# One encoder step in an order written out by a planner: first weight loads with places of their own, a margin for deferrable products, and measured durations in the planner's model

## The chip, the cores and the metric

The kernel runs on one core of a Trainium2 chip. The metric is the device time of that core in microseconds (us), as the median of several runs; the profile is one further execution, taken with the hardware profiler. TensorE (PE) multiplies, VectorE (DVE), ScalarE (ACT) and GpSimd (POOL) work on rows, SyncE (SP) issues all transfers.

## The reference, cut to what matters

One layer for 512 prompt tokens and 32 sample tokens, with 256 memory tokens, all in 32-bit floats. There are three head groups: A attends to a band of chunks, B to the highest-scored keys only, M to the memory. Cut down, for one sequence:

```python
def layer(x, mem, g, w_in, w_mem_kv, w_out, pos):
    z = _rmsnorm(x, g) @ w_in                       # 1024 -> 3880 columns, split:
    qa, ka, va, ga, qb, kb, vb, gb, qm, gm, qi, ki, wi = _split_cols(z)
    qb, kb, qi, ki = rope(qb), rope(kb), rope(qi), rope(ki)
    mk, mv = split(_rmsnorm(mem, g_mem) @ w_mem_kv)
    oa = softmax(qa @ ka.T / 8 + rel_bias) @ va     # 6 heads x 64, own chunk and 8 before
    score = sum_h(wi[h] * relu(qi[h] @ ki.T))       # 8 heads x 32, one shared key
    top = top_k(score, 128)                         # prompt; 256 for the sample
    ob = softmax(qb @ kb[top].T / 8) @ vb[top]      # 6 heads x 64
    om = softmax(qm @ mk.T / 8) @ mv                # 4 heads x 64
    o = concat(oa * silu(ga), ob * silu(gb), om * silu(gm))
    return _rmsnorm(x + o @ w_out, g_final)         # and all new keys and values
```

The sample attends to cached keys (1024 rows for B, 512 for A) beside its own 32.

## The kernel before, in words

Each product of the projections is done as three products of rounded halves: the inputs are split into a high and a low part (xTh, xTl; wh, wl), and TensorE adds wh·xTh, wh·xTl and wl·xTh in one bank. A weight piece arrives by a transfer (raw, four places), ACT rounds it (wh), POOL subtracts (wl). The 32 sample rows are done straight from raw and xF (w_sample), with no split.

Nothing is scheduled by a compiler: the Python program lays down every engine's instructions in the order in which they shall run. A class Line keeps a modelled clock for each engine and for the transfers, with a duration for each operation (cost, L62), a lag between engines (lag, L87) and the time at which each tile is written (had). The steps of the kernel are generators; each yields the model's time at which it wants to go on, for instance `line.at(tile)` (L169), the time at which the tile is ready plus a margin of 0.3. Between the products of the big projections (EARLY, then LATE, then out_part) the planner runs every generator whose time has come on TensorE's modelled clock. So the projections are the filler, and the other steps go in where the model says that their inputs are there. All operations go through one wrapper and therefore carry the same line, L233; they are told apart by the names of their tiles.

The steps that matter here: `start` (L656) issues the first transfers in the order of the string START (w: allow one more weight piece, x: a piece of x turned, t: the tables for rotation, r: 128 rows of x in natural order for the norms, m: memory). w_load (L409) lets a weight piece into one of four places when the piece four before it has been split. rows_load (L590) has two places for the rows (nat) and waits for the norm of the rows two before. norms gives rs, one over the root mean square of each row, on which the sparse branch and every rotation hang. `index` (L752) starts the sparse branch when all rows are normed: index_sample and index_prompt turn keys and queries (rot, stk, KS, QS; KSs, QSs for the sample), multiply them, and add the eight heads on VectorE (ysel for the prompt, ysS for the sample). picks then takes the 128 highest of each prompt row in 48 pairs of MAX8 and MATCH_REPLACE on VectorE. sample_choice finds the 256th highest score of each sample row by 22 rounds of trial: VectorE writes trial values (bi_neg, later bf_try), ACT counts what lies above (junkS, then bf_ok), TensorE adds up the counts (bank<-bf_ok,over), and VectorE takes the next digit (bi_ok, later bf_m and bf_cut). The last six rounds (bf_) settle ties. Group B's attention needs picks and choice; its products and the whole output projection come behind them.

The order of a queue is fixed, so an instruction that waits holds up all those behind it on its engine.

Of the kernel before, what the change touches and what calls it, by code (L numbers as in the profile page):

```python
# [17 lines left out]
P = 128  # L18
S = 512
# [16 lines left out]
START = "wxwxwxwtwwrrrrwwrmmrr"  # L36
# [7 lines left out]
class Line:  # L44
# [4 lines left out]
    def __init__(self):  # L49
        self.clk = dict.fromkeys(("PE", "DVE", "ACT", "POOL", "SP", "DMA"), 0.0)  # L50
        self.ready, self.used = {}, {}
        self.boxes = {}
        self.tables = {"exp": (AF.Exp, AF.Tanh)}
        self.table = None
        self.tasks = []
        self.seq = 0
        self.margin = 0.3
        self.time = 0.0
        self.window, self.busy, self.slow = 0.0, 0.0, True
        self.warm = None  # L60

    def cost(self, eng, op, outs, ins, kw):  # L62
        if eng == "PE":
            w = 1 if ins[0].dtype in (F32R, BF16) else 2 if op == "transpose" else 4
            n = outs[0].free_size() * w / 2400.0
            if op == "matmul" and ins[0].dtype == F32R:
                return 0.003 + max(n, 0.104) if "tile_position" not in kw else 0.02 + 0.5 * max(n, 0.104)
            if "tile_position" in kw:
                return 0.04 + n * (0.25 if outs[0].shape[0] == T else 0.5)
            return 0.003 + n  # L70
# [16 lines left out]
    def lag(of, to):  # L87

        if of == to or of is None:
# [49 lines left out]

    def op(self, eng, op, outs, ins, kw):  # L140
# [3 lines left out]
        if eng == "SP":  # L144
            self.clk[eng] = t + 0.05
            t = max(t + 1.1, self.clk["DMA"])
            end = t + outs[0].size() * 4 / 360e3
            self.clk["DMA"] = end
        else:
            d = self.cost(eng, op, outs, ins, kw)  # L150
            if eng == "PE":
                d = self.array(t, d)
            end = t + d
# [15 lines left out]
    def at(self, *tiles):  # L169
        return max(self.had(x) for x in tiles) + self.margin  # L170

# [91 lines left out]
def hybrid_step(ctx: ExitStack, tc: tile.TileContext, a: dict):  # L263
# [47 lines left out]
    ka = cp.tile([P, NT, 384], F32, tag="ka", name="ka")  # L311
    va = cp.tile([P, NT, 384], F32, tag="va", name="va")
# [6 lines left out]
    ysS = cp.tile([P, PAST + T], F32, name="ysS")  # L319
# [125 lines left out]
    def w_sample():  # L445
        for nm, i, n in parties:
            yield from line.wait(lambda: len(raws) > i + 1 and x_done[0] > 1)
            yield line.at(xF[:, 0:4, :], raws[i + 1])
            yield from room()
            p = bank()  # L450
            for j in (0, 2):
                yield from line.wait(lambda: len(raws) > i + j + 1 and x_done[0] > j + 1)
                yield line.at(raws[i + j], raws[i + j + 1], xF[:, 2 * j:2 * j + 4, :])
# [4 lines left out]
            yield line.at(p)  # L458
            if nm in ("kb", "vb"):
                yield from line.wait(lambda: 0 in over)  # L460
            out = (cp.tile([T, 384], F32, tag={"kb": "kaS", "vb": "vaS"}.get(nm, nm + "S"), name=nm + "S") if nm != "i"
                   else ix.tile([T, n], F32, name="zS"))
            A.copy(out, p[0:T, 0:n])
            for q in range(1, 4):
                yield line.at(out) - 0.2
                V.tensor_tensor(out, p[q * T:(q + 1) * T, 0:n], out, op=ALU.add)
            give(p)
            yield from line.wait(lambda: NT in normed)
            yield max(line.at(rs[0:T, NT:NT + 1]), line.at(out) - 0.2)
            V.tensor_scalar(out, out, rs[0:T, NT:NT + 1], None, op0=ALU.mult)  # L470
            news[nm] = out
            if nm in ("kb", "qb"):
                rope(out.rearrange("p (h d) -> p h d", d=64), out, T, 6, 64, ctab["cos64S"], ctab["sin64S"], V)
# [116 lines left out]
    def rows_load():  # L590
# [27 lines left out]
    def spread():  # L618

        yield from line.wait(lambda: NT in normed)  # L620
        yield line.at(rs)
# [130 lines left out]
    def index():  # L752
        nonlocal ip, identR
        yield from line.wait(lambda: len(indexed) == NT and NT in normed)
        p1.close()
        ip = pool(ipx, "ip", "right")
        identR = ip.tile([P, P], F32R, name="identR")
        V.tensor_copy(identR, ident)
# [39 lines left out]
    def index_prompt():  # L798
# [5 lines left out]
        yield line.at(kst)  # L804
# [7 lines left out]
        for t in range(1, NT):  # L812
            n = P * (t + 1)
            yield line.at(qst[t])
# [11 lines left out]
            yield line.at(QS)  # L826
# [16 lines left out]
    def index_sample():  # L843
# [14 lines left out]
        yield line.at(qsS)  # L858
# [14 lines left out]
        yield line.at(kst2)  # L873
# [5 lines left out]
        for k0, n in ((0, 512), (512, 512), (1024, T)):  # L879
            yield line.at(KSs)  # L880
# [7 lines left out]
            yield line.at(*rs)  # L888
# [33 lines left out]
    def sample_choice():  # L922
# [13 lines left out]
        def passed(of, bias, least_, scale=1.0):  # L936
# [4 lines left out]
            yield line.at(okf) - 0.2  # L941
# [137 lines left out]
    natural = {"ka": ka, "va": va}  # L1079

    def projections(order):
        for nm in order:
# [17 lines left out]
            else:  # L1100
                if nm not in natural:

                    line.until(lambda: (2 if nm == "kb" else 0) in over)
                    natural[nm] = cp.tile([P, NT, 384], F32, tag=nm, name=nm)
                of = f"new_{nm[1]}_{nm[0]}"
# [3 lines left out]
    def sample(mix, nh, nb, kt, cv, qT, kn, vn, pts, zin):  # L1109
# [6 lines left out]
        if kn is not None:  # L1116
            yield line.at(kn)
# [7 lines left out]
        yield line.at(qT, *kt)  # L1125
        yield from room(3)
        o_ps = bank()
        for g0 in range(0, nh, 4):
# [35 lines left out]
            yield line.at(z)  # L1164
# [18 lines left out]
            yield line.at(*(x[0] for x in blocks))  # L1183
            yield line.at(*cv)
# [94 lines left out]
    def turned_pair(nat, hp, then):  # L1279

        w = nat.shape[1] * P
        yield line.at(nat[:, :, hp * P:(hp + 1) * P])
# [55 lines left out]
    class Masked:  # L1338
# [57 lines left out]
        def turn(self):  # L1396
            pts = []
            for e in range(2):
                yield from line.wait(lambda: places[self.w] > 0)
                places[self.w] -= 1  # L1400
                yield line.at(self.z[e])
# [41 lines left out]
    def attend(i):  # L1443
# [9 lines left out]
        yield line.at(*pair.q, *pair.k)  # L1453
# [12 lines left out]
        yield line.at(*pts)  # L1466
# [220 lines left out]
```

## Time and profile before

| | us |
|---|---|
| median of 3 runs | 384.17 (383.58 to 387.33) |
| the profiled execution | 385.51 |
| its span in the trace | 383.7 |
| TensorE busy | 362.8 (95%) |
| VectorE busy | 286.1 (75%) |
| ScalarE busy | 224.5 (59%) |
| GpSimd busy | 186.1 (49%) |

The share of busy time is a mean over stages that have different limits, so it is to be read stage by stage. Matmuls of TensorE overlap, so a stage's busy time is the union of them, and the duration of one is read from the distance between starts. The mean granted clock of TensorE is 0.984 of full speed (2.4 GHz); its lower level is 1.2 GHz.

### The profile page before, as it was taken

Reading aid. Unit: us, or ns where it says so; the run is one execution under the profiler, and the core shown is the slowest. Engines: PE = TensorE matmul, PEld = TensorE weight load, DVE = VectorE, ACT = ScalarE, POOL = GpSimd, SP = SyncE. Lnnn points to the kernel's source line nnn. Section 1 sums busy time; section 2 is a strip of 40 time slices with the busy share of each in tenths; the row PEclk is TensorE's granted clock in tenths of the full one; section 3 lists DMA queues with packets and bytes.
Section 4 is the critical chain, followed back from the end, with each engine's and each line's share of the span. In section 5 each row is a group of like instructions: output and inputs, shape, how many; then the busy total and the mean of one; then the engine's idle time right before and its main releaser. Section 6 shows DMA issues by size and latency. Waiting matters only on the chain.

```text
span 383.7 us, 7976 instructions
## 1 busy us (share of the span) xinstructions
PE 362.8 (95%) x2961; PEld 324.6 (85%) x2961; DVE 286.1 (75%) x721; ACT 224.5 (59%) x529; POOL 186.1 (49%) x199
## 2 busy tenths in 40 slices
PE   8997889999999999999898999799999999999992
PEld 8795768999989888898697888799999877999992
DVE  3664877988999999999999997787755587422453
ACT  5664946898677777756475674323654556411353
POOL 1778862377433665416668623735224310633552
PEclk9999989999999999999998999989999999999998
DMA  7969641156564422112401220522145940230005
GB/s 248 309 209 290 194 140 58 61 172 186 166 205 141 124 72 57 42 42 80 114 24 61 85 63 27 164 56 55 43 156 195 370 167 2 78 140 4 0 15 219
DMA packets 41478, 46.35 MB, mean 121 GB/s; under 512 B 5184, under 2 KB 36544, under 8 KB 41440
## 3 DMA queue, kind: packets, MB, share of 16 engines
q1 hardware_dynamic: 41440, 45.85, 38.0%
q8 instruction: 23, 0.38, 0.4%
q14 instruction: 15, 0.12, 0.1%
HBM read 39.67 MB, written 6.16 MB: 119 GB/s over the span
## 4 chain that ended last, share of the span: by engine, by line
PE 67%; DVE 21%; DMA 5%; ACT 3%; issue 2%; SPq 1%; POOL 1%; POOLq 0%; DVEq 0%; ACTq 0%
PE bank L233 67%; DVE ysel L233 3%; DVE m L233 2%; DMA g_mem<-in_norm_mem_g_dram 2%; DVE z L233 2%; DMA raw<-in_w_in_dram 2%; DVE rank L233 1%; DVE st L233 1%; DVE rt L233 1%; DVE qbS L233 1%; SPq L233 1%; DMA cbi<-in_cache_b_kidx_dram 1%; DVE kbS L233 1%; ACT sq L233 1%; DVE rot L233 1%
## 5 line engine op out<-in xcount | busy, mean ns | idle before, releaser
L233 POOL TENSOR_TENSOR wl<-raw,wh 128x512 fp32r<-128x512 f32 (+2 forms) x68 | 107.7, 1592 | 116.0 <-ACT wh L233 105.6
L233 ACT ACTIVATE wh<-raw 128x512 fp32r<-128x512 f32 (+2 forms) x70 | 49.5, 715 | 43.4 <-PE bank L233 18.1
L233 PE MATMUL bank<-wh,xTh 128*128 128x384 f32 (+1 forms) x192 | 67.9, 354 | 0.0
L233 PE MATMUL bank<-wl,xTh 128*128 128x384 f32 (+1 forms) x192 | 64.9, 338 | 1.8 <-POOL wl L233 1.7
L233 PE MATMUL bank<-wh,xTl 128*128 128x384 f32 (+1 forms) x192 | 64.7, 337 | 0.0
L233 ACT ACTIVATE z<-z,st 128x256 f32<-128x256 f32 (+3 forms) x73 | 39.0, 548 | 23.9 <-DVE st L233 23.9
L233 PE MATMUL bank<-xTh,wh 128*128 128x272 f32 x208 | 46.5, 304 | 0.4 <-DVE st L233 0.4
L233 PEld LDWEIGHTS bank<-wh,xTh 128*128 128x128 f32 x192 | 37.3, 194 | 7.4 <-issue 6.5
L233 PE MATMUL bank<-xTl,wh 128*128 128x272 f32 x208 | 43.0, 288 | 0.0
L233 PE MATMUL bank<-xTh,wl 128*128 128x272 f32 x208 | 42.9, 288 | 0.0
L233 PEld LDWEIGHTS bank<-wl,xTh 128*128 128x128 f32 x192 | 37.2, 194 | 2.6 <-POOL wl L233 2.2
L233 PEld LDWEIGHTS bank<-wh,xTl 128*128 128x128 f32 x192 | 37.3, 194 | 0.4 <-DVE xTl L233 0.3
L233 PEld LDWEIGHTS bank<-xTh,wh 128*128 128x128 f32 x208 | 32.6, 189 | 3.1 <-issue 1.8
L233 PEld LDWEIGHTS bank<-xTl,wh 128*128 128x128 f32 x208 | 32.6, 188 | 0.0
L233 PEld LDWEIGHTS bank<-xTh,wl 128*128 128x128 f32 x208 | 32.6, 189 | 0.0
L233 PE MATMUL bank<-ident,z 128*128 128x128 f32 (+1 forms) x161 | 26.0, 281 | 1.7 <-ACT pt L233 1.1
L233 DVE TENSOR_TENSOR xr<-bank,xr 128x256 f32<-128x256 f32 (+1 forms) x24 | 12.3, 512 | 19.8 <-PE bank L233 19.7
L233 DVE MAX8 m<-ysel 128x8 f32<-128x256 f32 (+2 forms) x48 | 26.3, 548 | 0.0
L233 DVE MATCH_REPLACE8 ysel<-m,ysel 128x256 f32<-128x256 f32 (+2 forms) x48 | 26.0, 543 | 0.0
L233 PEld LDWEIGHTS bank<-ident,z 128*128 128x128 f32 (+1 forms) x161 | 18.0, 142 | 5.8 <-issue 2.1
L233 ACT ACTIVATE junkS<-ysS,bi_neg 128x1056 int8<-128x1056 f32 x16 | 18.8, 1177 | 3.6 <-DVE bi_neg L233 3.6
L233 ACT COPY pt<-bank 128x512 f32<-128x512 f32 (+1 forms) x28 | 14.8, 539 | 8.8 <-PE bank L233 8.7
(308 smaller groups left out, 902.2 us busy)
## 6 DMA issues: line engine op xcount, KB each, us to landing
raw<-in_w_in_dram SPq DMA_DIRECT2D x20, 384.0 KB, 3.5
raw<-in_w_in_dram SPq DMA_DIRECT2D x26, 256.0 KB, 2.9
raw<-in_w_out_dram SPq DMA_DIRECT2D x8, 384.0 KB, 3.2
nat<-in_x_prompt_dram SPq DMA_DIRECT2D x4, 512.0 KB, 5.3
raw<-in_w_mem_kv_dram SPq DMA_DIRECT2D x8, 256.0 KB, 2.8
xr<-in_x_prompt_dram SPq DMA_DIRECT2D x4, 512.0 KB, 5.6
out_dram<-xr SPq DMA_DIRECT2D x4, 512.0 KB, 2.6
xr<-in_x_t_dram SPq DMA_DIRECT2D x3, 544.0 KB, 6.1
```

Source lines behind the costliest of these rows:

```text
L233: return fn(*args, **kw)
```

## The change

- START has four weight pieces (w) ahead of the prompt's rows (r) instead of two. The first four pieces get places of their own (in the later places of q0 and gate0), and pieces below the eighth wait for no split. The rows from the third on get places of their own instead of taking turns in two; the tiles ka, va and ysS, whose places they use, are opened later (two waits in `projections` and `index` for that).
- `line.sure` (ready plus 1.0) stands in place of `line.at` (ready plus 0.3) before products of TensorE that nobody needs at once: in w_sample, spread, the indexer, the attention, and the rounds of the choice. A free bank is taken 0.4 later.
- What w_sample does behind its product goes into a generator of its own.
- The model: other durations for TensorE's operations, with one for a change of the array's division; VectorE and POOL wait for each other in the model where both use the port that they share; a transfer is given 1.6 instead of 1.1 before it lands and 330 instead of 360 GB/s.

```diff
-START = "wxwxwxwtwwrrrrwwrmmrr"
+START = "wxwxwxwtwwwwrrrrrmmrr"
+SURE = 1.0
...
-            n = outs[0].free_size() * w / 2400.0
-            if op == "matmul" and ins[0].dtype == F32R:
-                return 0.003 + max(n, 0.104) if "tile_position" not in kw else 0.02 + 0.5 * max(n, 0.104)
...
+            n = outs[0].free_size()
+            fast = ins[0].dtype in (F32R, BF16)
+            if op == "transpose":
+                d = max(0.085 if fast else 0.109 * ins[0].shape[0] / P, 0.06)
+            elif fast:
+                d = max(n / 2400.0 + 0.013, 0.107 if n > 1 else 0.04)
+            else:
+                d = 2 * max(n / 1190.0, 0.058)
...
+            if mode != self.mode:
+                self.mode = mode
+                d += 0.095 + (0.104 if fast else 0.056) * mode[1] / P
...
+    def port(self, eng, t, d):
+
+        for s, end, by in self.taken:
+            if by != eng and s <= t < end:
+                t = end
+        self.taken = [x for x in self.taken[-40:]] + [(t, t + d, eng)]
+        return t
...
+    def sure(self, *tiles):
+
+        return max(self.had(x) for x in tiles) + SURE
...
-            t = sorted(pp.free(f"b{b}") for b in free_banks)[k - 1]
+            t = sorted(pp.free(f"b{b}") for b in free_banks)[k - 1] + 0.4
...
-            yield from line.wait(lambda: allowed[0] > i and len(split) > i - 4 and (i - 4 not in party or i - 4 in met))
-            yield wp.free("raw")
-            raw = wp.tile([P, nk, hi - lo], F32, tag="raw", name="raw", bufs=4)
+            yield from line.wait(lambda: allowed[0] > i and (i < 8 or len(split) > i - 4 and (i - 4 not in party or i - 4 in met)))
+            if i < 4:
+
+                if i % 2 == 0:
+                    first = cp.tile([P, 2, nk, hi - lo], F32, tag=("q0", "gate0")[i // 2], name="raw")
+                raw = first[:, i % 2]
+            else:
+                yield wp.free("raw")
+                raw = wp.tile([P, nk, hi - lo], F32, tag="raw", name="raw", bufs=4)
...
-        if i <= NT:
-            yield from line.wait(lambda: len(normed) > i - 2)
+        if i < 2:
             t = rp.tile([P, D], F32, tag="nat", name="nat", bufs=2)
         else:
-            t = cp.tile([P, D], F32, tag=("rank", "gate0")[i - NT - 1], name="nat")
+            if i > NT + 1:
+                yield from line.wait(lambda: all(i in met for i in range(4)))
+            t = cp.tile([P, D], F32, tag=("ka", "va", "ysS", "rank", "gate0")[i - 2], name="nat")
...
-            yield line.at(okf) - 0.2
+            yield line.sure(okf)
```

SP's queue at the first loads of columns of 384 (raw is a weight piece, nat are rows of x or of the memory, mr the memory turned), before:

```order
L233 DMA sin32S<-in_sin_dram 32x32
L233 DMA raw<-in_w_in_dram 128x2x384 x2
L233 DMA nat<-in_x_prompt_dram 128x1024 x4
L233 DMA raw<-in_w_in_dram 128x2x384 x2
L233 DMA nat<-in_x_sample_dram 32x1024
L233 DMA mr<-in_mem_t_dram 128x4x256 x2
```

and of the change:

```order
L271 DMA sin32S<-in_sin_dram 32x32
L271 DMA raw<-in_w_in_dram 128x2x384 x4
L271 DMA nat<-in_x_prompt_dram 128x1024 x4
L271 DMA nat<-in_x_sample_dram 32x1024
L271 DMA mr<-in_mem_t_dram 128x4x256 x2
L271 DMA nat<-in_mem_prompt_dram 128x1024 x2
```

Two weight pieces moved from behind the prompt's rows to before them; the sample's rows have the same loads ahead of them as before.

VectorE in the last six rounds of the choice, ahead of the fourth (bf_m, bf_cut and bf_try are one round's; rt and kb are rotation, z softmax, o the gated output), before:

```order
L233 TENSOR_SCALAR bf_try<-bf_dig,bf_cut 128x1
L233 MAX m_78<-ysel_75 128x8
L233 MATCH_REPLACE ysel_75<-m_78,ysel_75 128x512
L233 TENSOR_SCALAR ysel_75<-ysel_75 128x512
L233 TENSOR_TENSOR rt<-bank,sin_125 128x384
L233 TENSOR_TENSOR kb<-bank,cos_123 128x384
```

and of the change, ahead of the fourth of the six rounds, as above:

```order
L271 TENSOR_SCALAR bf_try<-bf_dig,bf_cut 128x1
L271 TENSOR_TENSOR qbS<-bank,qbS 32x384 x3
L271 TENSOR_SCALAR qbS<-qbS,rs 32x384
L271 TENSOR_TENSOR rt<-qbS,sin64S 32x384
L271 TENSOR_TENSOR qbS<-qbS,cos64S 32x384
L271 TENSOR_TENSOR qbS<-rt,qbS 32x384
L271 SCALAR_TENSOR_TENSOR o<-bank,gate 128x256
L271 TENSOR_SCALAR bf_m<-bank 128x1
```

A pick (MAX, MATCH_REPLACE and a scaling behind it) stood ahead of the fourth of the last six rounds; before, seven of the 48 picks stand behind the first of these rounds, and of the change none does.

TensorE around the last of the 22 sums (xTh_86 or xTh_82 is one half of x's high parts), before:

```order
L233 MATMUL bank<-wh,xTl_88 128x384
L233 MATMUL bank<-wl,xTh_86 128x384
L233 LDWEIGHTS over_364
L233 MATMUL bank<-bf_ok,over_364 128x1
L233 MATMUL bank<-wh,xTh_86 128x384
```

and of the change:

```order
L271 MATMUL bank<-wl,xTh_82 128x384
L271 MATMUL bank<-raw,xF 32x384 x4
L271 MATMUL bank<-wh,xTh_82 128x384
L271 MATMUL bank<-wh,xTl_84 128x384
L271 MATMUL bank<-wl,xTh_82 128x384
L271 MATMUL bank<-wh,xTh_82 128x384
L271 MATMUL bank<-wh,xTl_84 128x384
L271 MATMUL bank<-wl,xTh_82 128x384
L271 LDWEIGHTS over_400
L271 MATMUL bank<-bf_ok,over_400 128x1
L271 MATMUL bank<-wh,xTh_82 128x384
```

Behind this last sum stood 44 products each of wh·xTh, wh·xTl and wl·xTh with 384 columns, and of the change stand 60 of each; all other products behind it are the same in number.

## Rows read from the trace of the kernel before

**Rows 1.** Busy time by stage; columns: stretch, its length, each engine, clock, DMA share, GB/s:

```profile
core 0: us, PE busy (x) PEld busy (x) DVE busy (x) ACT busy (x) POOL busy (x), PEclk, DMA share, GB/s
0.00:52.20 52.20, 45.80 (x290) 40.77 (x291) 32.23 (x53) 33.23 (x62) 35.42 (x61) 0.98 0.77 242
52.20:74.80 22.60, 22.46 (x139) 18.73 (x139) 17.06 (x40) 14.30 (x37) 7.64 (x9) 0.97 0.21 68
74.80:246.30 171.50, 166.36 (x1405) 147.74 (x1405) 159.08 (x435) 116.70 (x288) 92.87 (x84) 0.99 0.34 102
246.30:376.00 129.70, 127.96 (x1129) 117.27 (x1128) 75.52 (x193) 58.15 (x142) 48.70 (x42) 0.99 0.31 102
```

**Rows 2.** VectorE in order of time: start, duration, operation, [idle before <- releaser]:

```profile
74.77 0.42 DVE L233 MAX8 m<-ysel 128x8 f32<-128x256 f32 x1
...
246.08 0.21 DVE L233 TENSOR_SCALAR bf_try<-bf_dig,bf_cut 128x1 f32<-128x1 f32 x1
248.24 0.16 DVE L233 TENSOR_SCALAR bf_m<-bank 128x1 f32<-128x1 f32 x1 [1.94 <-PE bank L233]
```

**Rows 3.** VectorE's waits, 74.8 to 246.3: us in total, times, longest:

```profile
DVE ysel L233 <- ACT r L233: 2.1, 2, 1.3
DVE rt L233 <- POOL kb L233: 1.7, 2, 1.1
...
DVE bf_try L233 <- ACT oMh L233: 0.5, 1, 0.5
```

**Rows 4.** TensorE's waits, 74.8 to 246.3, first and last of six:

```profile
PE bank L233 <- ACT z L233: 1.3, 1, 1.3
...
PE bank L233 <- DVE z L233: 0.3, 1, 0.3
```

**Rows 5.** TensorE in order of time around the last sum of the choice:

```profile
242.69 0.34 PE L233 MATMUL bank<-wl,xTh 128*128 128x384 f32 x1
...
245.31 0.34 PE L233 MATMUL bank<-wl,xTh 128*128 128x384 f32 x1
248.04 0.16 PE L233 MATMUL bank<-bf_ok,over 128*128 128x1 bf16 x1 [2.39 <-ACT bf_ok L233]
...
248.32 0.52 PE L233 MATMUL bank<-wh,xTl 128*128 128x384 f32 x1
...
251.53 0.43 PE L233 MATMUL bank<-wl,xTh 128*128 128x384 f32 x1
```

**Rows 6.** SP's queue in order of time: start, time from first to last issue:

```profile
13.99 9.52 SPq L233 DMA_DIRECT2D nat<-in_x_prompt_dram  x4
...
26.53 0.33 SPq L233 DMA_DIRECT2D nat<-in_x_sample_dram  x1
```

**Rows 7.** TensorE's waits, 0 to 74.8: us in total, times, longest:

```profile
PE bank L233 <- POOL wl L233: 1.7, 2, 1.1
PE bank L233 <- POOL nhalf L233: 1.4, 1, 1.4
PE bank L233 <- DVE KSs L233: 1.1, 1, 1.1
PE bank L233 <- POOL rs L233: 1.1, 1, 1.1
PE bank L233 <- DVE ka L233: 0.7, 1, 0.7
PE bank L233 <- DVE stk L233: 0.3, 1, 0.3
```

**Rows 8.** VectorE's groups by shape, 74.8 to 246.3: busy us, mean ns | idle before:

```profile
L233 DVE TENSOR_SCALAR z<-z,st 128x256 f32<-128x256 f32 x12 | 7.4, 654 | 0.1
...
L233 DVE TENSOR_TENSOR gate<-bank,rb 128x272 f32<-128x272 f32 x12 | 4.7, 430 | 0.0
...
L233 DVE TENSOR_TENSOR rt<-bank,sin 128x384 f32<-128x384 f32 x4 | 2.2, 554 | 1.7 <-POOL kb L233 1.7
...
L233 DVE TENSOR_TENSOR qbS<-rt,qbS 32x384 f32<-32x384 f32 x1 | 2.1, 2081 | 0.0
L233 DVE TENSOR_SCALAR z<-z,st 128x512 f32<-128x512 f32 x4 | 2.1, 536 | 0.1
```

More of the change, by code (lines that the diff above doesn't have):

```diff
@@ L54, in __init__ @@
         self.table = None
+        self.mode = None
+        self.taken = []
         self.tasks = []
@@ L87, in lag @@
     def lag(of, to):
+        if of is None and to == "PE":
+            return 0.3
         if of == to or of is None:
@@ L138, in array, with shares @@
         return d
+    @staticmethod
+    def shares(op, outs, ins):
+        if outs[0].space == PSUM or any(x.space == PSUM for x in ins):
+            return False
+        full = [x for x in ins if x.free_size() > 1]
+        if op in ("scalar_tensor_tensor", "tensor_tensor"):
+            return True
+        return op in ("tensor_scalar", "tensor_copy") and len(full) > 0 and outs[0].dtype == F32
+    def port(self, eng, t, d):
[4 more added lines that the diff above has]
+        return t
     def op(self, eng, op, outs, ins, kw):
@@ L145, in op @@
             self.clk[eng] = t + 0.05
-            t = max(t + 1.1, self.clk["DMA"])
-            end = t + outs[0].size() * 4 / 360e3
+            t = max(t + 1.6, self.clk["DMA"])
+            end = t + outs[0].size() * 4 / 330e3
             self.clk["DMA"] = end
@@ L152, in op @@
                 d = self.array(t, d)
+            elif eng == "POOL" or eng == "DVE" and self.shares(op, outs, ins):
+                t = self.port(eng, t, d)
             end = t + d
@@ L457, in w_sample, with sample_rows @@
                 met.extend((i + j, i + j + 1))
[L458 to L473, printed above, removed]
+            line.spawn(sample_rows(nm, n, p))
+    def sample_rows(nm, n, p):
+        yield line.at(p)
+        if nm in ("kb", "vb"):
+            yield from line.wait(lambda: 0 in over)
+        out = (cp.tile([T, 384], F32, tag={"kb": "kaS", "vb": "vaS"}.get(nm, nm + "S"), name=nm + "S") if nm != "i"
+               else ix.tile([T, n], F32, name="zS"))
+        A.copy(out, p[0:T, 0:n])
+        for q in range(1, 4):
+            yield line.at(out) - 0.2
+            V.tensor_tensor(out, p[q * T:(q + 1) * T, 0:n], out, op=ALU.add)
+        give(p)
+        yield from line.wait(lambda: NT in normed)
+        yield max(line.at(rs[0:T, NT:NT + 1]), line.at(out) - 0.2)
+        V.tensor_scalar(out, out, rs[0:T, NT:NT + 1], None, op0=ALU.mult)
+        news[nm] = out
+        if nm in ("kb", "qb"):
+            rope(out.rearrange("p (h d) -> p h d", d=64), out, T, 6, 64, ctab["cos64S"], ctab["sin64S"], V)
     def tokens(acc, xh, xl, w, c, t, c0, c1, first, last):
@@ L752, in index @@
     def index():
-        nonlocal ip, identR
-        yield from line.wait(lambda: len(indexed) == NT and NT in normed)
+        nonlocal ip, identR, ysS
+        yield from line.wait(lambda: len(indexed) == NT and NT in normed and all(i in met for i in range(4)))
         p1.close()
@@ L879, in index_sample @@
         for k0, n in ((0, 512), (512, 512), (1024, T)):
-            yield line.at(KSs)
+            yield line.sure(KSs)
             yield from room(2)
@@ L1077, in memory @@
         return group_n(mTh, mTl, 256, NM // P, done, finish, NT + 1, m_done)
-    natural = {"ka": ka, "va": va}
+    natural = {}
     def projections(order):
+        nonlocal ka, va
         for nm in order:
@@ L1101, in projections @@
                 if nm not in natural:
-                    line.until(lambda: (2 if nm == "kb" else 0) in over)
+                    line.until(lambda: NT - 1 in normed if nm[1] == "a" else (2 if nm == "kb" else 0) in over)
                     natural[nm] = cp.tile([P, NT, 384], F32, tag=nm, name=nm)
+                    ka, va = (natural.get(n) for n in ("ka", "va"))
                 of = f"new_{nm[1]}_{nm[0]}"
@@ L1124, in sample @@
             give(p)
-        yield line.at(qT, *kt)
+        yield line.sure(qT, *kt)
         yield from room(3)
@@ L1182, in sample @@
                 blocks += [(pt, b, i, w) for b, i, w in bw]
-            yield line.at(*(x[0] for x in blocks))
-            yield line.at(*cv)
+            yield line.sure(*(x[0] for x in blocks))
+            yield line.sure(*cv)
             for j0 in range(0, len(hs), 2):
@@ L1452, in attend @@
             pair.q, pair.k = yield from pair.prep()
-        yield line.at(*pair.q, *pair.k)
+        yield line.sure(*pair.q, *pair.k)
         yield from room(2)
```

39 lines of the change are left out of this document (19 added, 20 removed).

## The prediction

> **What bounds the kernel now.** I read the engines' busy time by stage first, then what each engine waited for in each stage, then single instructions. The stages [rows 1] show three limits in turn. Up to 52.2 us nobody is full: TensorE is busy 45.8 us of 52.2, VectorE 32.2, and the DMA share is 0.77. From 52.2 to 74.8 TensorE is full (22.46 of 22.60). From 74.8, the first of the 48 picks (MAX8), to 246.3, the end of the last trial value (bf_try) of the sample's choice [rows 2], **both** engines look full: TensorE 166.4 of 171.5 us, VectorE 159.1. From 246.3 on TensorE alone is: 128.0 of 129.7, and VectorE has 75.5 us of work in it. What is left of the span, 7.7 us, is a tail that the change leaves alone.
>
> Which of the two full engines sets the middle stage? VectorE's named waits there are five groups, 6.2 us in all, from "ysel on r" with 2.1 to "bf_try on oMh" with 0.5 [rows 3]; the other 6.2 us between busy time and stage are gaps between one instruction and the next. TensorE's named waits are six groups, 4.2 us, from "z" with 1.3 to "z by VectorE" with 0.3 [rows 4]. But TensorE's work in this stage can be chosen: it is filled with projection products that nobody needs yet, and those left over are done after 246.3, where it has no other limit. VectorE's cannot: 384 instructions stand on it between the first pick and the last trial value, and the choice is not over before them. At the stage's end TensorE does stand still for the choice: it ends its products at 245.6 and waits 2.39 us for bf_ok [rows 5]. So I take VectorE as the limit of this stage.
>
> Behind the choice the bound is simply how many products TensorE has left. The time is therefore: start of the picks, plus VectorE's work from there to the last trial value, plus TensorE's work left behind it, plus a fixed tail.
>
> **The change, part by part.** *Early loads.* Four weight loads go ahead of the prompt's rows on SP's queue instead of two, with places of their own, and the rows no longer share two buffers. Now the sample's rows are issued at 26.53, after a stretch of 9.52 us in which four row loads wait for places [rows 6]; the sparse branch needs them (through rs). The same bytes stand ahead of them as before (four weight pieces, four row loads), so it is only the waits for places that go. TensorE's waits before the first pick, apart from the 1.4 us for nhalf at the start (untouched), are wl 1.7, KSs 1.1, rs 1.1, ka 0.7, stk 0.3 [rows 7]. The longest wl wait, 1.1, is the second half of the weight pieces that come after the rows, and ka is a store to a place that is opened later now. I take 1.1 + 1.1 + 1.1 + 0.7 + 0.3 = 4.3 us off. Behind the waits the granted clock fell to the lower level: after the wait for bf_ok ten steps from product to product take 251.53 − 248.32 = 3.21 us, where ahead of it fifteen take 245.31 − 242.69, 0.175 each at the upper level [rows 5]. That is 1.5 us lost; the early stretch, with a mean clock of 0.98 up to 52.2 and 0.97 behind it [rows 1], has one such fall too, and I let its 1.5 us go with the waits. VectorE has 85 instructions ahead of the first pick instead of 91; six at about 0.2 (the small ones, as bf_try's 0.21 [rows 2]) are 1.3 us. In the order the eighth product of keys and queries stands where it stood, behind the same TensorE work, so nothing is given back there. Sum **−7.1 us** for the first pick. Bounds: −3, when only the clock and the first wl wait go and the rest turn up again one step on; −10, when the 1.4 us of nhalf and half of the early gaps of VectorE go too.
>
> *VectorE's work from the first pick to the last trial value* grows from 384 to 394 instructions. By the rows of like instructions [rows 8]: three gate products come from POOL's list, 3 × 0.43; one more round of the sign search, three small instructions of 0.2, 0.6; two more and one less softmax scaling of about 0.6, +0.6; one addition of keys from POOL, 0.55; four rotation products go behind the last trial value, −4 × 0.55. Sum **+0.9 us**, bounds 0 and +2.
>
> *TensorE's work behind the last bf_ok.* The order is plain here: behind that row stood 44 of each of the three 384-column products, now 60 of each. That is 48 products more, at 0.175 us [rows 5] **+8.4 us**; everything else behind it is the same list. The total of TensorE's work is the same to two small products, so this is no added work but work moved from before the choice's end to behind it. Where it was, VectorE was the limit and it cost nothing; where it is, TensorE is alone and it costs all. Bounds: +8.4 if TensorE then still has no wait behind the choice (now none is named), +6.9 if the 1.5 us at the lower clock there go.
>
> *The margin.* Deferrable products now go out 1.0 us after their input is ready by the order's reckoning instead of 0.3, and a bank is taken 0.4 later. Each moves a wait of TensorE to a wait of nobody, as long as there are fillers; it makes everything that VectorE needs from such a product up to 0.7 us later. No row prices that. VectorE's waits of 6.2 us [rows 3] are what a better fitted order could remove; TensorE reaching each step with less work ahead of it could add as many. I take half off, **−3.1 us**, since the picks now stand closer together and give VectorE work that needs nobody; bounds −6.2 and +6.
>
> Sum: −7.1 + 0.9 + 8.4 − 3.1 = **−0.9 us**. The profiled execution took 385.51 us (a span of 383.7 and 1.8 around it), 1.3 above the median of the runs, 384.17; against that median the forecast is **383.3 us**: no change that can be told.
>
> **The rivals.** *VectorE without waits, and a full early gain.* All 6.2 us of waits go and the picks begin 10 us earlier: −2.9 and −3.1 more, **377.3 us**. For it: the early waits hang together, and one that goes takes those behind it along. Against it: three of the five groups in [rows 3] hang on ACT and POOL, whose work doesn't shrink. Chance 0.17.
>
> *The port.* Some VectorE instructions last longer than their size explains: the sample's rotation of 32 x 384 takes 2.08 us against 0.55 for one of 128 x 384 that reads PSUM, and a scaling of 256 columns 0.65 against 0.54 for one of 512 [rows 8]. With two such rotation steps (2 × 1.5) and 12 × 0.11 at least 4.3 us of VectorE's middle stage are of this kind. The order now reckons with them; if it thereby parts them, **379.0 us**. Against it: it only reckons, no rule in it picks the free moment, and POOL's list of splits is as long as before. Chance 0.13. The Trainium skill, "SBUF — State Buffer", section "Who interferes with whom", says that VectorE and GpSimd share a pair of ports as an exclusive lock, and "Issue order, not op shape, decides who blocks". By that rule the same list of instructions can cost VectorE nothing or a whole POOL instruction each time, so it allows this gain and as large a loss; the long rotation beside the short one agrees with it.
>
> *Slower: rounds without cover.* A round of the choice goes VectorE, ACT, TensorE, VectorE. In the last round now nothing stood between: VectorE waited 1.94 us for TensorE's sum, and TensorE 2.39 for ACT [rows 2, 5]. Before the change seven picks stand among the last five rounds as cover; after it none, they are all earlier. And TensorE has 8.4 us less work ahead of the last bf_ok, so it comes to these rounds early and stands still, and what VectorE would have done in between (rotations, scalings) is queued behind the waiting product. It decides from three uncovered rounds of the five on: 3 to 4 × 1.94 = 5.8 to 7.8 us instead of the 3.1 gained, halfway for what the order still puts between them: +6 us, **389 us**. Against it: the order still has four or more VectorE instructions in each of those five rounds. Chance 0.14.
>
> *The change doesn't do what it says.* The first loads are not what the early stage waits for: 0.77 of the DMA engines are busy, and the queue's 13.99 to 23.51 can be their speed and not the places [rows 1, 6]. Then the picks begin 3 us earlier and no more, and the 8.4 us behind stays: **387.4 us**. Chance 0.10.
>
> **How the numbers follow.** The forecast's own case has 0.46, with 380 to 387 as its own range. A measurement of this kernel can tell about 1% (3.8 us) from no change, so faster is below 380.3 and slower above 388.0. Faster: 0.17 and 0.13 of the first two rivals, 0.03 of the forecast's lower end: 0.33. Slower: 0.14, 0.04 of the last rival, 0.03 of the upper end: 0.21. Within: 0.46. The range reaches to the first two rivals and to the slower one, 376.5 to 389.5, and leaves their far sides out.
>
> **What the profile after would show.** Right: the first MAX8 at 67 to 68 us; the last bf_try near 237; VectorE's named waits between them about 3 us; behind the last bf_ok about 136 us of TensorE without a wait; six or so us of waits of TensorE *before* it, on bf_ok, z or pt. Wrong: if TensorE shows no waits in the middle stage although 8.4 us of its work is gone from it, VectorE was faster than I reckoned, and the time is that of the first two rivals; if bf_m waits for TensorE in several rounds, it is the slower one; if the first MAX8 stands at 72, the last.

## The result, and the profile after

The changed kernel takes 387.97 us (median of 20 runs) against 385.22 us for the kernel before (20 runs): 1.0075 times as long, 95% interval 1.0051 to 1.0098. So it is slower, by 0.75%, where 383.3 us and no change were forecast. The time of the forecast's last rival (387.4 us) is the one that came. Single executions of several of these kernels took 430 us or more (up to 1912 us); the medians and ratios in this document leave them out, and e5 and g1, whose profiles were taken in such executions, have no rows. The profiled execution of the changed kernel took 391.14 us, the longest of the 20, with a mean granted clock of 0.974; two kernels below, with the same order up to the middle stage, show what a usual one does.

Busy time by stage, changed kernel, columns as in [rows 1]; the cuts are at its own first pick and last trial value:

```profile
0.00:52.20 52.20, 47.66 (x303) 42.71 (x303) 29.97 (x52) 30.68 (x56) 33.16 (x58) 0.93 0.75 238
52.20:72.35 20.15, 19.22 (x116) 16.69 (x116) 15.61 (x33) 14.02 (x36) 8.62 (x11) 1.00 0.26 86
72.35:243.37 171.02, 161.72 (x1357) 142.67 (x1357) 158.16 (x445) 118.33 (x288) 80.82 (x74) 0.98 0.33 95
243.37:381.70 138.33, 137.06 (x1194) 125.89 (x1192) 75.87 (x198) 58.84 (x142) 59.07 (x52) 1.00 0.32 105
```

VectorE's two marks in it (start, duration; against [rows 2]):

```profile
72.35 0.42 DVE L271 MAX8 m<-ysel 128x8 f32<-128x256 f32 x1
...
243.16 0.21 DVE L271 TENSOR_SCALAR bf_try<-bf_dig,bf_cut 128x1 f32<-128x1 f32 x1
```

The picks start 2.4 us earlier than in [rows 2] (74.77 to 72.35), the way from there to the end of the last trial value is 171.0 us against 171.5, and from there to the end of the span 146.0 against 137.4. −2.4 − 0.5 + 8.6 = +5.7 us, which is the difference of the spans (389.4 and 383.7). Told in TensorE's terms the same 5.7 us are 2.8 us more busy time (365.7 against 362.8, for nearly the same list of products, 2965 records against 2961, so lower clock) and 2.9 us more standing still (23.7 against 20.9). The lower clock belongs to this execution and not to the change: over its 20 runs the median of the mean clock is 0.987, and over the runs of the kernel before beside the experiments it is about 0.982. So a usual execution of the change loses its time by standing still. An estimate from these numbers: busy 365.7 × 0.974 / 0.987 = 361 us of a span of 386, so 25 us of standing still, 4 more than before. What TensorE waited for over the whole span of the profiled execution (us in total, times, longest; against [rows 4, 7]):

```profile
PE bank L271 <- POOL rs L271: 2.8, 1, 2.8
PE bank L271 <- ACT z L271: 2.7, 2, 2.0
PE bank L271 <- DVE pt L271: 1.9, 2, 1.2
PE bank L271 <- ACT bf_ok L271: 1.8, 1, 1.8
PE bank L271 <- POOL nhalf L271: 1.4, 1, 1.4
...
PE bank L271 <- DVE gate L271: 0.2, 1, 0.2
```

The thirteen groups are 14.4 us together; the list of before has 12.9 (with [rows 5]).

The loads did move. SP's queue (against [rows 6]):

```profile
14.41 1.88 SPq L271 DMA_DIRECT2D nat<-in_x_prompt_dram  x4
16.34 0.47 SPq L271 DMA_DIRECT2D nat<-in_x_sample_dram  x1
```

The sample's rows are issued at 16.34 instead of 26.53. But rs, the norms that they are for, is no earlier. ScalarE and then POOL in order of time, changed kernel:

```profile
24.19 0.17 ACT L271 COPY wI<-bank 128x8 f32<-128x8 f32 x1 [1.60 <-PE bank L271]
...
28.55 1.06 ACT L271 ACTIVATE junk<-nat 32x1024 bf16<-32x1024 f32 x1
```

```profile
17.04 5.42 POOL L271 TENSOR_TENSOR wl<-raw,wh 128x768 fp32r<-128x768 f32 x3
...
30.72 0.57 POOL L271 TENSOR_TENSOR rs<-ss,nhalf 128x1 f32<-128x1 f32 x1
...
33.78 1.05 POOL L271 TENSOR_TENSOR rs<-ss,nhalf 32x1 f32<-32x1 f32 x1
```

The same two instructions on the sample's row in the kernel before:

```profile
31.14 1.06 ACT L233 ACTIVATE junk<-nat 32x1024 bf16<-32x1024 f32 x1 [1.84 <-DMA nat<-in_x_sample_dram]
```

```profile
33.97 1.02 POOL L233 TENSOR_TENSOR rs<-ss,nhalf 32x1 f32<-32x1 f32 x1
```

ScalarE squares the sample's row at 28.55, 2.6 us earlier than before, and POOL, which has three weight splits and then all small steps of the norms in one row, comes to it at 33.78 instead of 33.97. TensorE's product of it waits 2.8 us (before 1.1, [rows 7]), and behind this wait the clock falls: 0.93 in this stage against 0.98 in [rows 1]. In e3 and e4 below, with the same early order, it is 0.97 there, so most of that fall is this execution's. All named waits of TensorE before the first pick are 5.4 us here and 5.5 in e4; before they were 6.3 [rows 7].

### The profile page after: what moved, and what is told of

Its sections match the earlier page's. It is cut to its first block, busy times and chain, and to the rows that moved or that the text cites. A ratio compares the mean times of both kernels' runs of the same rounds, so it can differ in the third digit from the quotient of the medians.

```text
span 389.4 us, 7975 instructions
## 1 busy us (share of the span) xinstructions
PE 365.7 (94%) x2965; PEld 328.0 (84%) x2965; DVE 281.7 (72%) x729; ACT 224.0 (58%) x523; POOL 182.5 (47%) x195
## 4 chain that ended last, share of the span: by engine, by line
PE 51%; DVE 30%; DMA 7%; ACT 5%; issue 4%; POOL 2%; SPq 1%; POOLq 0%; DVEq 0%; ACTq 0%
PE bank L271 51%; DVE ysel L271 8%; DVE m L271 5%; DVE z L271 5%; DMA g_mem<-in_norm_mem_g_dram 2%; DMA nat<-in_x_prompt_dram 2%; DMA cos<-in_cos_dram 2%; DVE tmpA L271 1%; POOL ss L271 1%; DVE pt L271 1%; ACT sq L271 1%; DVE gate L271 1%; DVE queried L271 1%; DMA xr<-in_x_t_dram 1%; DVE bi_thr L271 1%
## 5 line engine op out<-in xcount | busy, mean ns | idle before, releaser
L271 ACT ACTIVATE wh<-raw 128x512 fp32r<-128x512 f32 (+2 forms) x70 | 49.8, 716 | 43.4 <-PE bank L271 20.9
L271 PE MATMUL bank<-xTh,wh 128*128 128x272 f32 x208 | 48.0, 310 | 1.3 <-ACT z L271 0.7
L271 DVE SCALAR_TENSOR_TENSOR ysel<-r,wI,ysel 128x256 f32<-128x256 f32 (+2 forms) x21 | 21.1, 1003 | 4.2 <-ACT r L271 3.4
```

What stands on the lines that cost most here:

```text
L271: return fn(*args, **kw)
```

## The experiments

All ratios are against the kernel before on the same chip, with 95% interval; the time is the median. "Behind" is the number of 384-column products behind the last bf_ok, read from each order. Waits are the sum of TensorE's named waits, the clock is the mean over the span, both of the profiled execution; the last trial value is where VectorE starts it.

| kernel | us | ratio | behind | last trial value | waits | clock |
|---|---|---|---|---|---|---|
| before | 385.2 | | 132 | 246.1 | 12.9 | 0.984 |
| the change (loads, model, margin) | 388.0 | 1.0075 (1.0051 to 1.0098) | 180 | 243.2 | 14.4 | 0.974 |
| e1 loads | 378.3 | 0.9795 (0.9767 to 0.9823) | 144 | 232.9 | 7.8 | 0.988 |
| e2 model | 392.9 | 1.0169 (1.0135 to 1.0202) | 246 | 227.1 | 18.0 | 0.976 |
| e5 margin | 385.8 | 1.0011 (0.9991 to 1.0031) | 18 | | | |
| e6 loads, margin | 385.8 | 0.9999 (0.9970 to 1.0028) | 18 | 272.7 | 15.3 | 0.981 |
| e7 loads, model | 392.2 | 1.0186 (1.0147 to 1.0224) | 246 | 224.5 | 17.5 | 0.979 |
| e8 model, margin | 392.6 | 1.0189 (1.0151 to 1.0228) | 180 | 244.8 | 13.0 | 0.972 |
| f1 loads, TensorE's durations | 393.1 | 1.0204 (1.0172 to 1.0236) | 240 | 229.4 | 16.5 | 0.979 |
| g3 the same without division | 383.2 | 0.9934 (0.9900 to 0.9967) | 138 | 242.0 | 12.0 | 0.987 |
| f2 loads, port | 377.6 | 0.9808 (0.9785 to 0.9832) | 132 | 225.1 | 7.7 | 0.997 |
| f3 loads, transfers and 0.3 us | 389.0 | 1.0102 (1.0078 to 1.0126) | 210 | 230.1 | 15.9 | 0.989 |
| g4 loads, transfers | 385.2 | 0.9985 (0.9954 to 1.0017) | 150 | 239.7 | 12.4 | 0.985 |
| f4 loads, margin but for the choice | 375.7 | 0.9754 (0.9725 to 0.9784) | 108 | 244.9 | 8.3 | 0.984 |
| g1 the change, choice's margin old | 392.5 | 1.0187 (1.0139 to 1.0236) | 222 | | | |
| g2 loads, port, margin but for the choice | 373.5 | 0.9679 (0.9643 to 0.9715) | 66 | 244.5 | 7.1 | 0.997 |

In this table the time goes with the waits, and it goes as well with the number behind: e5 and e6 (18) aside, it is 373.5 us at 66 and 388 us or more in all seven kernels with 180 or more. So "more products behind the choice" is a rival to "more waits" as what makes a kernel slow; e4 below bears on it.

**e1, the early loads alone**: START, the places of the first loads, and `sample_rows`; the rest of the diff undone.

```diff
-START = "wxwxwxwtwwrrrrwwrmmrr"
+START = "wxwxwxwtwwwwrrrrrmmrr"
```

> The kernel before with the early loads alone (the string START, the places of the first weight pieces and of the rows, the rest of the sample's product in a generator of its own); model, margin and bank rule as before. Behind the last bf_ok stand 144 products of 384 columns (before 132, changed kernel 180). Theory 1 (the early loads buy only some 2 us, because the norms' chain on ScalarE and GpSimd and not the loads gates the sparse branch; VectorE limits the middle stage; every product moved behind the choice costs 0.175 us): first MAX8 2 to 3 us earlier than before, then 12 x 0.175 = 2.1 us more behind the choice: the time of before, within 1 us. Theory 2 (TensorE is as full in the middle stage as behind it, so where a product stands costs nothing, and the change's loss is new waits and lower clock of TensorE): 2 us faster than before, since 1.9 us of its idle time before 52 us goes.

2% faster: more than either theory had, nearer to theory 2. The early stage loses its waits:

```profile
PE bank L233 <- DVE kb L233: 1.8, 1, 1.8
PE bank L233 <- DVE bf_m L233: 1.6, 1, 1.6
PE bank L233 <- POOL nhalf L233: 1.4, 1, 1.4
PE bank L233 <- ACT r L233: 0.6, 1, 0.6
...
```

These are the first four of its groups of TensorE's waits. No wait for rs, KSs or ka is left; TensorE has other products there, although POOL starts rs of the sample's row only at 35.28, later than before (33.97). The first pick is at 69.51, 5.3 us earlier. The middle stage is 7.9 us shorter (163.6 instead of 171.5), and the way behind it 5.7 us longer. In total the loads alone are worth what was forecast for them (7.8 us against 7.1), but not by the way that was forecast, which had all of it before the first pick; what loses it again is the rest of the change.

**e2, the model's figures alone**: the new `cost`, `lag`, `shares`, `port` and the transfers' figures; START, places and margins as before.

> The kernel before with the model's new durations, port and transfer figures alone; loads, margin and bank rule as before. Behind the last bf_ok stand 246 products of 384 columns, 114 more than before, 66 more than in the changed kernel. Theory 1 (VectorE limits the middle stage, products behind the choice cost): the choice ends at most a few us earlier than before, so 114 x 0.175 = 20 us come on top: 400 us or more. Theory 2 (TensorE full everywhere, its work is the same): the choice's last sum stands about 20 us earlier on TensorE, and the time is that of before within 2 us, apart from new waits.

1.7% slower, 7 us and not the 20 of theory 1; theory 2 has the time of before apart from new waits. The choice ends 19 us earlier than before and the time is longer all the same: with 114 more products behind, TensorE waits 18.0 us instead of 12.9.

**e3 and e4, 7 us of TensorE's work left out** of the changed kernel, in the middle stage or behind the choice, every other instruction in its place (line.op only reckons with the product, it doesn't issue it).

```diff
-                        PE.matmul(acc[j][:, 0:H], w[:, kk, :], x[c][:, kk, j * H:(j + 1) * H], start=first, stop=last)
+                        if 0 < line.rounds < 22 and x is xTl and line.seen % 3 == 0 and line.left_out < 56:
+                            line.op("PE", "matmul", [acc[j][:, 0:H]], [w[:, kk, :], x[c][:, kk, j * H:(j + 1) * H]], {})
...
-            PE.matmul(o, l, wh[:, kk, c0:c1], start=False, stop=False)
+            if line.rounds == 22 and line.left_out < 40 and c1 - c0 == 384:
+                line.op("PE", "matmul", [o], [l, wh[:, kk, c0:c1]], {})
...
```

> The changed kernel with 56 of the products wh x xTl of 272 columns left out of the middle stage (every third between the first and the last sum of the choice); every other instruction stands where it stood. The outputs lack those parts. Theory 1 (VectorE limits the middle stage): the choice ends when it did, TensorE only waits more: within 1 us of the changed kernel (388.0). Theory 2 (TensorE is the limit there too): 56 x 0.12 = 6.7 us faster, 381 us.

> The changed kernel with 40 of the products wh x xTl of 384 columns left out behind the last sum of the choice; every other instruction stands where it stood. The outputs lack those parts. Both theories: 40 x 0.175 = 7.0 us faster than the changed kernel, 381 us, since TensorE alone is the limit there; a smaller gain would mean that another engine is near the limit behind the choice too.

e3 took 388.5 us (ratio 1.0059, 1.0031 to 1.0086) and e4 388.5 (1.0062, 1.0035 to 1.0088): **neither gains** anything clear: against the change's 1.0075 that is 0.6 and 0.5 us less, and the intervals leave room for 2 us at most. In the middle stage that was theory 1. Behind the choice it contradicts both, and my "TensorE alone". What e4's TensorE waited for from 243.3 to 386.8, where the changed kernel has no named wait:

```profile
PE bank L272 <- DMA raw<-in_w_in_dram: 2.3, 2, 1.8
PE bank L272 <- POOL qb L272: 1.7, 1, 1.7
```

With the work gone TensorE runs into the weight pieces, which come when SP's queue has waited for POOL's splits, and into POOL's rotation of qb. These waits are 4.0 of the 7.0 us; from 253 to 263 us the clock is 0.83, where the changed kernel has 1.00 (by an estimate 1.7 us more); and the stage from the last trial value to the end takes 145.9 us instead of 146.0. Named waits are 19.2 us over the span instead of 14.4. So 7 us of products less is next to no time less: at this place another queue is late by about as much as TensorE is busy. The 40 products are the first ones behind the choice, up to 264 us, so the run says nothing of the rest of that stage. In e3 the same waits as in the changed kernel grow, ACT z from 2.7 to 3.9 us and bf_ok from 1.8 to 3.4. Both have the first pick at 70.4 to 70.8, so in a usual execution of the change the picks start some 4 us earlier than in [rows 2], not 2.4.

**e5 to e8, the other combinations of the three parts.**

> The kernel before with the margin alone (1.0 instead of 0.3 before deferrable products, and a bank taken 0.4 later); loads and model as before. Behind the last bf_ok stand 18 products of 384 columns instead of 132. Theory A (the three parts add up: loads alone -7.8, model alone +6.8, all three +2.8, so the margin has +3.8): 389.5 us. Theory B (each edit gives a new order whose waits and port conflicts are a new draw, and the parts don't add): anything from 380 to 392; a sum that misses by more than 3 us in two of these four runs speaks for it.

> Early loads and margin, the model as before; 18 products of 384 columns behind the last bf_ok. Theory A: 385.7 - 7.8 + 3.8 = 382 us. Theory B: not bound to that; if the early stage's gain is the loads' own, the first MAX8 is at 70 us or earlier whatever the time.

> Early loads and the model's new figures, the margin as before; 246 products of 384 columns behind the last bf_ok. Theory A: 385.7 - 7.8 + 6.8 = 385 us. Theory B: not bound to that.

> The model's new figures and the margin, the loads as before; 180 products of 384 columns behind the last bf_ok, as in the changed kernel. Theory A: 385.7 + 6.8 + 3.8 = 396 us. Theory B: not bound to that. In both the difference to the changed kernel (388) is what the early loads are worth under the new order; if that is far from 7.8, the model takes the loads' gain away.

Theory A falls: e5 to e8 miss its sums by 3.7, 3.8, 7.2 and 3.4 us. In e6 the first MAX8 is at 72.5 us and not at 70 or earlier, so the early gain isn't the loads' own whatever the order. The loads are worth 2.1% alone, nothing with the margin or with the model, and 1.1% (1.0189 to 1.0075) where both are there. Theory B's mark is met, but the model is slower in each of the four pairs, by 0.8 to 4.0%, where mere chance would have both signs.

**f1 to f4, g3, g4: the parts of the model and of the margin, each with the early loads.** f1:

```diff
+            if mode != self.mode:
+                self.mode = mode
+                d += 0.095 + (0.104 if fast else 0.056) * mode[1] / P
```

with the other new durations of TensorE (g3 leaves these three lines out); f2 `shares` and `port`; f3 the two edits below, g4 the second alone; f4 `line.sure` everywhere but at okf, where `line.at(okf) - 0.2` stays.

```diff
+        if of is None and to == "PE":
+            return 0.3
...
-            t = max(t + 1.1, self.clk["DMA"])
-            end = t + outs[0].size() * 4 / 360e3
+            t = max(t + 1.6, self.clk["DMA"])
+            end = t + outs[0].size() * 4 / 330e3
```

> Early loads, and of the model's new figures only the durations of TensorE's operations with the charge for a change of the array's division; 240 products of 384 columns behind the last bf_ok (early loads alone: 144). Theory C (the harm is in TensorE's durations: the order then puts fewer fillers between a step and the next, TensorE comes to the steps before their inputs and waits): 391 to 393 us, as with the whole model, and 15 us or more of named waits of TensorE against 7.8 with the early loads alone. Theory D (the harm is in the port's or the transfers' figures): 378 to 381 us.

> Early loads, and of the model's new figures only the port that VectorE and POOL share; 132 products of 384 columns behind the last bf_ok. Theory C: 378 to 381 us. Theory D: 385 us or more. If the port's reckoning parts the two engines' instructions, VectorE's long cases (rotation of 32 x 384 at 2 us, ysel at 1 us) become rarer and the time falls below 378 us.

> Early loads, and of the model's new figures only the transfers' (1.6 us and 330 GB/s) and the 0.3 us before TensorE may use a place that has come free; 210 products of 384 columns behind the last bf_ok. Theory C: 378 to 381 us. Theory D: 385 us or more. If the number of products behind the choice were itself the cost (0.175 us each), 378.3 + 66 x 0.175 = 390 us; if not, it stays near 378.

> Early loads and the margin, but the 22 rounds of the choice keep the old margin (bf_ok is used 0.1 us after it is ready by the model, not 1.0); model as before; 108 products of 384 columns behind the last bf_ok (with the margin in the rounds too: 18, and 385.8 us). Theory E (the margin takes the loads' gain away because it comes 22 times over in the choice's chain, 0.9 us each): 378 to 380 us. Theory F (the margin costs elsewhere, in the softmax and the eviction chains): 383 us or more.

> Early loads and TensorE's new durations without the charge for a change of the array's division; 138 products of 384 columns behind the last bf_ok (with the charge 240 and 393 us, without any new duration 144 and 378 us). If the charge is the harm: 377 to 381 us. If the products' durations are: 388 us or more.

> Early loads and the transfers' new figures (1.6 us, 330 GB/s), without the 0.3 us before TensorE uses a place that has come free; 150 products of 384 columns behind the last bf_ok (with the 0.3 us 210 and 389 us). If the 0.3 us is the harm: 377 to 381 us. If the transfers' figures are: 386 us or more.

TensorE's durations undo the loads' gain and more (0.9795 to 1.0204); two thirds of it is the charge for a change of division (1.0204 to 0.9934), the rest the products' durations. So theory C holds for f1 and f2; but f3 is as slow as theory D said, and g3 and g4 lie between their two cases. The transfers' figures cost 1.9%, the 0.3 us another 1.2%. The port costs nothing. f3's other case, 0.175 us for each product behind, has 390 us and 389.0 came, but the same sum gives 379 us for g4, which takes 385.2. f1's largest groups of TensorE's waits (twelve, 16.5 us in all):

```profile
PE bank L244 <- DVE gate L244: 3.1, 1, 3.1
PE bank L244 <- ACT bf_ok L244: 2.5, 4, 1.2
PE bank L244 <- DVE stk L244: 2.4, 2, 1.8
PE bank L244 <- POOL wl L244: 1.8, 3, 0.6
...
```

There is no single place: gate, bf_ok, stk, wl, each come a little late. That fits an order made with longer durations for TensorE: it is given fewer fillers between one step and the next, comes early, and waits. That this is the way is argued from these rows; no run here changed a duration downwards. An early choice is not the harm by itself: it ends at 225 to 230 us in e2, e7, f1 and f3, but also in f2 (225.1), which is among the fastest. f3's 2.6 us on bf_ok and 3.1 on rs belong to the same pattern.

The new durations are not simply too long. A product of 384 columns was 0.163 us in the model, is 0.173 now and takes 0.175 [rows 5]. And where TensorE goes from products of 64 rows back to those of 128, e4's trace shows

```profile
270.54 0.35 PE L272 MATMUL bank<-kl,q 64*128 64x384 f32 x2
270.81 0.44 PE L272 MATMUL bank<-wh,xTh 128*128 128x384 f32 x1
271.10 0.34 PE L272 MATMUL bank<-wh,xTl 128*128 128x384 f32 x1
271.27 0.34 PE L272 MATMUL bank<-wl,xTh 128*128 128x384 f32 x1
```

steps of 0.27 and 0.29 us and then the usual 0.17: some 0.21 us more for one such change, for which the new model charges 0.20.

f4 confirms theory E, with 375.7 us even below its 378 to 380: the margin outside the choice's rounds is no loss, and inside them it is (385.8 in e6, where the last trial value is only at 272.7).

**g1 and g2.**

> The full change, but the 22 rounds of the choice keep the old margin (0.1 us after bf_ok by the model instead of 1.0); 222 products of 384 columns behind the last bf_ok (changed kernel 180). Theory G (the model now draws the rounds too far forward, and the margin in them makes up for some of it): slower than the changed kernel, 391 us or more, with more than 14.4 us of named waits of TensorE. Theory H (the margin in the rounds is a cost in itself, as with the old model): 385 us or less.

> The parts that did no harm together: early loads, the port in the model, the margin outside the choice's rounds; 66 products of 384 columns behind the last bf_ok. If the gains add: 377.6 - 2.5 = 375 us. If each order is a draw of its own: 374 to 381 us.

g1 is theory G in its time: in the full change the margin in the rounds makes up for part of what the model does (392.5 without, 388.0 with it); its waits aren't known. g2, the parts that do no harm, takes 373.5 us, below both of its expected ranges, 3.2% less than before and 3.9% less than the change (0.9679 to 1.0075). Its stages, up to the first pick, to the last trial value, and to the end:

```profile
0.00:66.32 66.32, 63.27 (x409) 56.04 (x410) 43.67 (x77) 43.59 (x86) 40.49 (x63) 1.00 0.67 213
66.32:244.72 178.40, 174.11 (x1458) 155.98 (x1457) 165.22 (x464) 123.31 (x296) 93.61 (x87) 1.00 0.36 103
244.72:371.60 126.88, 119.57 (x1098) 109.70 (x1097) 71.87 (x188) 57.86 (x145) 47.89 (x48) 0.99 0.32 109
```

Its choice ends 1.4 us *later* than the changed kernel's, and it is 14.4 us faster. TensorE is busy 357.0 us in it instead of 365.7, with nearly the same products, at a clock of 1.00 instead of 0.93 in the early stage (0.97 in e3 and e4), and its named waits are 7.1 us.

## Why the prediction was wrong

Two steps failed. In the sum it was the first term, the early loads: 4.3 us of TensorE's waits before the first pick were to go and the clock's 1.5 with them; 0.9 us of waits went, and the clock up to 52.2 us fell (0.98 before, 0.93 in the profile, 0.97 in e3 and e4). Behind it the rule failed by which all terms were priced. And what makes the kernel slower had no term of its own: the model's new figures, which cost 1.7% alone (e2) and 0.8 to 4.0% in all four pairs.

**What bounds the kernel.** This is the rule: "start of the picks, plus VectorE's work from there to the last trial value, plus TensorE's work left behind it". As a sum over the trace it closes, as any cut does, and its third term was even met (+8.4 forecast, +8.6 measured). But it is no price list, so the third term's agreement is in part luck. The last trial value stands at 227 us in e2 (392.9 us) and at 244.5 in g2 (373.5); 40 products less behind the choice (e4) gave nothing. What goes with the time is TensorE's named waits: 7.1 to 8.3 us in the four kernels at 373 to 378 us, 12 to 19 in all others that have a profile. Among those others they don't rank the kernels (13.0 us at 392.6, 12.9 at 385.2), and the clock alone doesn't either (0.989 at 389.0, 0.984 at 375.7). As I read it, each in-order queue is late at some places and early at others, and what counts is how many of those places fall on TensorE. That is not shown: no run changed the waits alone, and the number of products behind the choice goes with the time about as well.

**The early loads, −7.1 us.** Mis-sized here: −2.4 in the profiled execution, some −4 in the usual one. Alone (e1) they give −5.3 at the first pick. I had rs hang on the sample's rows alone. The rows come 10 us earlier and rs only 0.2, as ScalarE's squares stand behind waiting copies and POOL's chain behind three splits. Nor does the first pick hang on rs: POOL starts it at 35.28 in e1 and 35.61 in g2, later than before, and their picks start at 69.5 and 66.3. What differs is whether TensorE has fillers meanwhile: its named waits before the first pick are 2.9 us in both, 6.3 before and 5.4 in the change, where the wait for rs grew from 1.1 to 2.8 us.

**VectorE's list, +0.9, and the margin, −3.1.** Together −0.5 was measured instead of −2.2. (The trace counts 435 and 445 VectorE instructions in the stage where the prediction has 384 and 394; the difference is the same.) VectorE's named waits in the middle stage stayed (6.0 us against 6.2), so the −3.1 has nothing to show for it. VectorE's long cases moved, as its groups by shape in the middle stage show (72.4 to 243.4 us, columns as in [rows 8]):

```profile
L271 DVE TENSOR_SCALAR z<-z,st 128x256 f32<-128x256 f32 x11 | 5.9, 563 | 0.1
...
L271 DVE TENSOR_SCALAR z<-z,st 128x512 f32<-128x512 f32 x4 | 3.5, 898 | 0.1
...
L271 DVE TENSOR_TENSOR qbS<-rt,qbS 32x384 f32<-32x384 f32 x1 | 0.5, 547 | 0.0
```

The sample's rotation fell from 2081 to 547 ns, and the scaling of 256 columns from 654 to 563, but that of 512 columns rose from 536 to 898 [rows 8]. VectorE's time over the stage is 0.9 us less (158.2 against 159.1) with ten instructions more, so of the 4.3 us of the port's rival at most a small part came. The Trainium skill, "SBUF — State Buffer", section "Who interferes with whom", has the port go to whoever issues first; that the same instruction takes 0.55 or 2.08 us by the order agrees with it. Reckoning with the port alone (f2) moved the time by 0.1%, from 0.9795 to 0.9808, within both intervals.

**The chances.** The rival that came, "the first loads are not what the early stage waits for", had 0.10, and its mechanism is half right: the wait is in POOL's and ScalarE's queues, and not in the transfers' speed (the four row loads are issued in 1.88 us instead of 9.52, so it had been their places). That its time came is luck too, as it adds the 8.4 us by the rule that failed. Of the signs named for the forecast's own case two came: no named wait of TensorE behind the choice, and some 7 us of them on z, pt and bf_ok before it. The slower rival (rounds without cover) did not come: its one wait for bf_ok (1.8 us) is in an early round, and bf_m has none in the last ones. Above all, new figures in a planner's model were costed by the instructions that they moved at one place, and they are a new order everywhere.

## What to carry to other kernels

Where several in-order queues are each nearly full, don't price a moved instruction by the stage it leaves and the one it enters: add up the waits of the fullest engine over the whole span as well, and look at more than one execution before the clock is made the reason. Take a change of three parts apart before judging it: here one part was worth −2.1%, one +1.7%, and the parts did not add. A planner's figure that is nearer to the truth by itself can make the order worse, and what one figure does hangs on the others: the margin in the choice's rounds costs with the old model (e6 against f4) and helps with the new one (the change against g1). So time each figure alone, and with the others.

## What was not expected of the hardware

Seven microseconds of matmuls taken out of an engine that is 94% busy gave 0.6 and 0.5 us back at two places (e3, e4). And part of the distance between the best and the slow kernels is clock: TensorE's busy time for nearly the same products is 357.0 us in g2 and 368.4 in e8, at a mean granted clock of 0.997 and 0.972.
